# The second layer norm of an encoder block: root and bias moved to a diagonal matrix product on TensorE

## The chip, the core and the metric

One NeuronCore of a Trainium2 chip runs the whole program: TensorE (PE) with its weight loads (PEld), VectorE (DVE), ScalarE (ACT), GpSimd (POOL) and SyncE (SP), which issues most DMAs. The metric is the device time of one execution in microseconds (us), as the median of several runs.

## What is computed

One encoder block on 1024 tokens of width 1024: token mixer, first layer norm, a mixture of 32 experts with two per token, and a second layer norm. The change touches only the last step:

```python
def _layer_norm(x, gain, bias):
    xf = x.astype(jnp.float32)
    mu = jnp.mean(xf, axis=-1, keepdims=True)
    var = jnp.mean(jnp.square(xf - mu), axis=-1, keepdims=True)
    y = (xf - mu) * lax.rsqrt(var + LN_EPS)
    return (y * gain.astype(jnp.float32) + bias.astype(jnp.float32)).astype(x.dtype)

x = _layer_norm(ALPHA * x + ffn, ln2_gain[layer], ln2_bias[layer])
```

## The kernel before

The experts add their rows to the tensor Y in DRAM with indirect DMAs from GpSimd (`scatter`, L1101). When the last of these has landed, a loop over experts' overflow blocks (L1152) runs zero times here, and SyncE loads Y back as eight tiles `zs[0]` to `zs[7]` of 128 tokens by 1024 columns (L1257). From there to the end of the program only the second norm runs.

Each tile passes through these steps. The queues of ScalarE and VectorE keep the order in which the code writes them (`manual_schedule`).

- Statistics. For tiles 0 and 4 (`DVE_STATS`) VectorE takes them: two `bn_stats` (L1278), `bn_aggr` (L1279), and the epsilon added (L1280). For the six others ScalarE passes over the tile twice: `sums(j, 0)` (L1268, mean) and `sums(j, 1)` (L1270, sum of squares about the mean); both write their unused result into the output tile `o`. VectorE then makes the variance of it with one small instruction (L1282).
- Reciprocal root. `first_root` has ScalarE make a first guess from the bits of the variance with Exp (L154) and square it (L155); VectorE refines it with four instructions of one column, each reading the one before (two at L156, then L157 and L158). The result is -16/5 of the root, which the gain's factor of -5/16 (L1258) makes good.
- `centred` (L1294): VectorE subtracts the mean and multiplies by the gain, in place, over 1024 columns.
- `finish` (L1301): VectorE multiplies by the root and adds the bias over 1024 columns, and SyncE writes the tile out (L1302); the last tile goes in two halves.

The loop of L1310 to L1325 interleaves them: the centring of tile a, the first statistics pass of tile a+2 on ScalarE, the variance and first root step of tile a+1, the second pass of tile a+2, and the finish of tile a. TensorE has no work after the last expert. The PSUM tag `gu` has three buffers of 128 by 512.

A matrix product of plain float32 operands is used by the router (`logits`, L820: 128 by 128 against 36 columns, eight per token tile) and, as a transpose against the identity, at L813 and L1029. The large products (`mm3`, L162 to L164) use operands of type fp32r, three products per pair.

Of the kernel before, what the change touches and what calls it, by code (L numbers as in the profile page):

```python
# [11 lines left out]
F32 = mybir.dt.float32  # L12
F32R = mybir.dt.float32r
BF = mybir.dt.bfloat16
I32 = mybir.dt.int32
AF = mybir.ActivationFunctionType
OP = mybir.AluOpType
# [6 lines left out]
D = 1024  # L24
# [43 lines left out]
Y_OUT = (6, 7)  # L68
COMB = ()
M4 = 4  # L70
LN2_ORDER = tuple(range(8))
DVE_STATS = (0, 4)
LN2_LAST = 7


C_ID = 0
# [30 lines left out]
def body(tc, ctx, A, out):  # L107
    nc = tc.nc
    PE, ACT, DVE, POOL, SP = nc.tensor, nc.scalar, nc.vector, nc.gpsimd, nc.sync
# [11 lines left out]
    def nm(s):  # L121
        uid[0] += 1
        return f"{s}{uid[0]}"

    def slot(shape, dt, name):
        return S.tile([128] + shape, dt, name=nm(name), tag="S", bufs=NS)
# [7 lines left out]
    def st(shape, name="st", dt=F32):  # L134
        return sm.tile([128] + shape, dt, name=nm(name), tag="st", bufs=8)
# [7 lines left out]
    def r(ap):  # L143
        return ap.bitcast(F32)

    def split(hi, lo, src):
        ACT.copy(hi, src)  # L147
        DVE.tensor_sub(lo, src, r(hi))  # L148

    def rsqrt_steps(y, x, q):  # L150


        return [
            lambda: (ACT.activation(y, x.bitcast(I32), AF.Exp, scale=-0.5 * LN2 / 2 ** 23, bias=rs_b),  # L154
                     ACT.activation(q, y, AF.Square)),  # L155
            lambda: (DVE.tensor_mul(x, x, q), DVE.scalar_tensor_tensor(q, x, -4.2, x, op0=OP.add, op1=OP.mult)),  # L156
            lambda: (DVE.scalar_tensor_tensor(q, q, 7.0, x, op0=OP.add, op1=OP.mult),  # L157
                     DVE.scalar_tensor_tensor(y, q, -7.0, y, op0=OP.add, op1=OP.mult)),  # L158
        ]
# [9 lines left out]
    ident = cst[:, C_ID:C_ID + 128]  # L169
# [22 lines left out]
    raws, halves = {}, {}  # L192
# [39 lines left out]
    for k in range(8):  # L232
# [9 lines left out]
        for m in range(4):  # L242
            for h in range(2):
                c, t = slice(m * 128, m * 128 + 128), slice(h * 512, h * 512 + 512)
# [16 lines left out]
    ang, n = pf[:, 0], pf[:, 1]  # L261
# [32 lines left out]
    def F(shape, name="f"):  # L294
        n = cur["f"] = cur["f"] + 1
        settle(("f", n - cur["nF"]))
        return cur["F"].tile([128] + shape, F32, name=nm(name), tag="F", bufs=cur["nF"])
# [211 lines left out]
    q = SP.dma_start(TAB, A["tab"])  # L509
# [145 lines left out]
    steps = [(h, i) for h in range(NH) for i in range(8)]  # L655
# [3 lines left out]
    for s in range(-2, len(steps)):  # L659
        h, i = steps[max(s, 0)]  # L660
        b = B[i]
        if s >= 0 and h < NH - 1:
            q = (h + 1) // 2
# [66 lines left out]
    for m in range(8):  # L730
# [6 lines left out]
        for h in range(2):  # L737
            t = slice(h * 512, h * 512 + 512)
            if m % 3 == 0 or m >= M4:
                ps = F([512], "pa")  # L740
            else:
                if h == 0:
                    pa = p3.tile([128, T], F32, name=nm("pa"), tag="S", bufs=2)
                ps = pa[:, t]
            for _ in rows(ps, ("wa", m), h, oT, h):
                pass
            x = st([512], "mt")
# [17 lines left out]
    for i in range(8):  # L765
        b = where["wo", i]
        for h in range(2):
            k, n = i // 4 * 4 + i % 2 * 2 + h, i // 2 % 2
            c = slice(h * 512, h * 512 + 512)
# [195 lines left out]
    with tc.manual_schedule(engines={mybir.EngineType.PE, mybir.EngineType.Activation}):  # L965
        for group in ((0, 1), (2,), (3,), (4,), (5,), (6, 7)):
# [3 lines left out]
            i = 0  # L970
# [24 lines left out]
    def mt(shape, name, dt, bufs):  # L995
        return mo.tile([128] + shape, dt, name=nm(name), tag=name, bufs=bufs)

    def rt(shape, name, dt, bufs):
        return mt(shape, name, dt, bufs)[:CAP]

    def pt(shape, name, bufs, rows=128):
        return p6.tile([128] + shape, F32, name=nm(name), tag=name, bufs=bufs)[:rows]
# [17 lines left out]
    def turn_to(n, name):  # L1020
        return mt([2, n, CAP], name, F32R, {8: XT_BUFS, 4: HT_BUFS}[n])
# [180 lines left out]
    with tc.manual_schedule(engines={mybir.EngineType.PE, mybir.EngineType.Activation, mybir.EngineType.DVE}):  # L1202
        x, h = turn_to(8, "xT"), rt([512], "h", F32, 1)
# [5 lines left out]
        for e in range(NE):  # L1209
# [20 lines left out]
            if e == 0:  # L1230
                x = x1
            elif e + 1 < NE:
                x = turn_to(8, "xT")
# [12 lines left out]
    ln2 = slot([2, D], F32, "ln2")  # L1246
# [5 lines left out]
    zs = []  # L1252
    for j in range(8):
        if j % 2 == 0:
            zp = slot([2, D], F32, "z")
        zs.append(zp[:, j % 2])
        SP.dma_start(zs[j], Y[j * 128:j * 128 + 128])  # L1257
    ACT.activation(ln2[:, 0], ln2[:, 0], AF.Copy, scale=-5.0 / 16)  # L1258
    warm = mt([1], "warm", F32, 1)
    ACT.activation(warm, eps, AF.Exp)  # L1260
    os, vs = {}, {}

    def sums(j, i):

        if j not in DVE_STATS:
            v, o = vs[j], os[j // 2][:, j % 2]
            if i == 0:
                ACT.activation(o, zs[j], AF.Copy, scale=1.0 / D, accum_out=v[:, 0:1])  # L1268
            else:
                ACT.activation(o, zs[j], AF.Square, bias=v[:, 0:1], scale=-1.0, accum_out=v[:, 4:5])  # L1270

    def variance(j):
        z, v = zs[j], vs[j]
        var = v[:, 1:2]
        if j in DVE_STATS:
            b = mt([12], "bn", F32, 2)
            for h in range(2):
                DVE.bn_stats(b[:, 6 * h:6 * h + 6], z[:, 512 * h:512 * h + 512])  # L1278
            DVE.bn_aggr(v[:, 0:2], b)  # L1279
            DVE.tensor_scalar(var, var, EPS, None, op0=OP.add)  # L1280
        else:
            DVE.tensor_scalar(var, v[:, 4:5], 1.0 / D, EPS, op0=OP.mult, op1=OP.add)  # L1282

    def halves(j):
        n = 2 if j == LN2_LAST else 1
        return [slice(i * (D // n), (i + 1) * (D // n)) for i in range(n)]

    def first_root(j):
        v = vs[j]
        vs[j, "r"] = steps = rsqrt_steps(v[:, 2:3], v[:, 1:2], v[:, 3:4])  # L1290
        steps[0]()

    def centred(j):
        DVE.scalar_tensor_tensor(zs[j], zs[j], vs[j][:, 0:1], ln2[:, 0], op0=OP.subtract, op1=OP.mult)  # L1294

    def finish(j):
        o, y = os[j // 2][:, j % 2], vs[j][:, 2:3]
        for s in vs[j, "r"][1:]:
            s()
        for c in halves(j):  # L1300
            DVE.scalar_tensor_tensor(o[:, c], zs[j][:, c], y, ln2[:, 1, c], op0=OP.mult, op1=OP.add)  # L1301
            SP.dma_start(out[j * 128:j * 128 + 128, c], o[:, c])  # L1302

    for j in range(8):
        if j % 2 == 0:
            os[j // 2] = slot([2, D], F32, "o")
        vs[j] = mt([5], "v", F32, 8)

    with tc.manual_schedule(engines={mybir.EngineType.Activation, mybir.EngineType.DVE}):
        j = LN2_ORDER + (None, None)  # L1310
        variance(j[0])
        sums(j[1], 0)
        first_root(j[0])
        sums(j[1], 1)
        for a in range(8):
            centred(j[a])
            if a < 6:
                sums(j[a + 2], 0)
            if a < 7:
                variance(j[a + 1])  # L1320
                first_root(j[a + 1])
            if a < 6:
                sums(j[a + 2], 1)
            finish(j[a])
    p6p.__exit__(None, None, None)  # L1325


# [88 lines left out]
```

## Time and profile before

| | us |
|---|---|
| median of 3 runs (lowest, highest) | 1566.15 (1562.53, 1566.98) |
| the profiled execution's own time | 1564.77 |
| its span, first to last instruction | 1563.0 |
| PE busy in the span | 1488.5 (95%) |
| DVE busy | 1195.1 (76%) |
| ACT busy | 945.3 (60%) |
| POOL busy | 277.3 (18%) |
| chip's granted TensorE clock, mean | 0.976 of full speed |

All times of rows count from the span's start. Shares are of the whole span, and stages differ: for the change only the last 45 us matter, in which TensorE does nothing. A spacing is the time from the start of one instruction to the start of the next on the same engine; a row's duration can be a little longer than the spacing, since the end of one instruction overlaps the start of the next. The granted clock is 1.00 for 2.4 GHz and 0.50 for 1.2 GHz.

### The profile page before, as it was taken

How to read it: one execution, taken by the hardware profiler on the slowest of the kernel's cores; microseconds unless marked ns; L12 is line 12 of the kernel's file. 1: busy time of each engine (PE TensorE's matmuls, PEld its weight loads, DVE VectorE, ACT ScalarE, POOL GpSimd, SP SyncE). 2: the span in 40 equal slices, each digit the busy share in tenths (PEclk: the TensorE clock that was granted, in tenths of full speed). 3: DMA queues.
4: the chain of work that ended last, by engine and by line, in shares of the span. 5: the costliest groups of instructions: out<-in, count | busy, mean ns of one | idle time of the engine just before them, and what ended most of it. 6: DMA issues, size and time to landing. Idle time of an engine off the chain costs nothing.

```text
span 1563.0 us, 22004 instructions
## 1 busy us (share of the span) xinstructions
PE 1488.5 (95%) x7627; PEld 1189.5 (76%) x7627; DVE 1195.1 (76%) x2284; ACT 945.3 (60%) x1571; POOL 277.3 (18%) x231
## 2 busy tenths in 40 slices
PE   8999999999999999999999988999999999999980
PEld 6988887798798898888888775777777777776750
DVE  5774214987988987775566788999989999898967
ACT  4323124665666766674341116888888888888864
POOL 0001000220210211100002544223222222211410
PEclk9999999999999999999999988999999999999995
DMA  6156224746856765618465477999999999999945
GB/s 237 56 175 201 81 75 101 222 152 170 231 184 176 215 188 144 150 67 312 150 256 208 171 261 256 383 370 375 375 374 356 362 364 357 366 352 377 396 147 215
DMA packets 116977, 375.46 MB, mean 240 GB/s; under 512 B 13767, under 2 KB 44871, under 8 KB 91504
## 3 DMA queue, kind: packets, MB, share of 16 engines
q1 hardware_dynamic: 76128, 303.25, 52.7%
q0 software_dynamic: 40160, 69.96, 17.3%
q8 instruction: 61, 1.00, 0.3%
q10 hardware_dynamic: 576, 0.83, 0.2%
q14 instruction: 52, 0.43, 0.1%
HBM read 312.44 MB, written 69.78 MB: 245 GB/s over the span
## 4 chain that ended last, share of the span: by engine, by line
PE 55%; issue 28%; POOL 9%; DVE 5%; ACT 1%; DMA 1%; POOLq 0%; DVEq 0%; SPq 0%; ACTq 0%
POOL Y L1101 7%; PE ps L570 4%; PE pg L162 4%; PE pg L163 4%; PE pg L164 4%; PE po L621 3%; PE pv L162 2%; PE pv L164 2%; PE pv L163 2%; PE tp L606 2%; POOL xg L1089 2%; PE pa L164 2%; PE pa L163 2%; PE pa L162 2%; PE pw L162 2%
## 5 line engine op out<-in xcount | busy, mean ns | idle before, releaser
L148 DVE TENSOR_TENSOR wh<-we,wh 128x1024 fp32r<-128x1024 f32 x384 | 459.7, 1219 | 54.1 <-ACT wh L147 50.5
L147 ACT CAST wh<-we 128x1024 fp32r<-128x1024 f32 x384 | 400.4, 1047 | 90.0 <-PE gu L164 51.5
L162 PE MATMUL gu<-wh,xT 128*96 128x512 f32 x512 | 204.3, 399 | 0.0
L164 PE MATMUL gu<-wh,xT 128*96 128x512 f32 x512 | 202.6, 396 | 0.6 <-DVE xT L148 0.6
L163 PE MATMUL gu<-wh,xT 128*96 128x512 f32 x512 | 201.8, 394 | 0.0
L1101 POOL DMA_INDIRECT Y<-y,idx x32 | 108.5, 3390 | 265.4 <-ACT y L1109 260.6
L148 DVE TENSOR_TENSOR w<-wraw,w 128x512 fp32r<-128x512 f32 x111 | 75.7, 685 | 92.1 <-ACT w L147 91.7
L147 ACT CAST w<-wraw 128x512 fp32r<-128x512 f32 x111 | 68.5, 621 | 115.1 <-PE pg L164 36.4
L573 ACT ACTIVATE P<-ps,stat 128x256 f32<-128x256 f32 (+7 forms) x128 | 94.8, 741 | 58.9 <-DVE stat L572 58.4
L164 PEld LDWEIGHTS gu<-wh,xT 128*96 128x96 f32 x512 | 83.0, 162 | 37.2 <-DVE xT L148 1.3
L163 PEld LDWEIGHTS gu<-wh,xT 128*96 128x96 f32 x512 | 83.3, 163 | 34.1 <-issue 0.5
L162 PEld LDWEIGHTS gu<-wh,xT 128*96 128x96 f32 x512 | 83.0, 162 | 33.2 <-ACT xT L147 0.2
L162 PE MATMUL dn<-wh,hT 128*96 128x512 f32 x256 | 102.4, 400 | 0.6 <-ACT hT L147 0.6
L570 PE MATMUL ps<-K,Q 128*128 128x512 f32 (+2 forms) x384 | 99.5, 364 | 1.2 <-DVE z L461 0.8
L164 PE MATMUL dn<-wh,hT 128*96 128x512 f32 x256 | 100.6, 393 | 0.0
L163 PE MATMUL dn<-wh,hT 128*96 128x512 f32 x256 | 100.6, 393 | 0.0
L162 PE MATMUL pg<-xT,w 128*128 128x512 f32 x256 | 100.4, 392 | 0.0
L163 PE MATMUL pg<-xT,w 128*128 128x512 f32 x256 | 100.0, 391 | 0.0
L164 PE MATMUL pg<-xT,w 128*128 128x512 f32 x256 | 99.9, 390 | 0.0
L572 DVE TENSOR_REDUCE stat<-ps 128x1 f32<-128x256 f32 (+7 forms) x128 | 95.3, 746 | 1.1
L570 PEld LDWEIGHTS ps<-K,Q 128*128 128x128 f32 x384 | 64.6, 189 | 10.8 <-DVE z L461 1.3
L162 PE MATMUL pv<-w,xT 128*128 128x256 f32 x256 | 72.8, 284 | 0.0
(277 smaller groups left out, 3395.3 us busy)
## 6 DMA issues: line engine op xcount, KB each, us to landing
we<-in_we_dram SPq DMA_DIRECT2D x192, 1024.0 KB, 23.5
wraw<-in_w_dram SPq DMA_DIRECT2D x61, 512.0 KB, 3.8
Q<-RQ POOLq DMA_DIRECT2D x64, 256.0 KB, 5.2
RQ<-rh SPq DMA_DIRECT2D x32, 256.0 KB, 3.3
K<-RK POOLq DMA_DIRECT2D x16, 512.0 KB, 5.5
V<-RV POOLq DMA_DIRECT2D x16, 512.0 KB, 5.7
OT<-ohl SPq DMA_DIRECT2D x48, 128.0 KB, 2.5
oT<-OT POOLq DMA_DIRECT2D x6, 1024.0 KB, 12.1
```

Of the source, the lines that this page charges most:

```text
L147: ACT.copy(hi, src)
L148: DVE.tensor_sub(lo, src, r(hi))
L162: PE.matmul(ps, a[0], b[0], start=start, stop=False)
L163: PE.matmul(ps, a[0], b[1], start=False, stop=False)
L164: PE.matmul(ps, a[1], b[0], start=False, stop=stop)
L570: PE.matmul(ps[:, c:c + n], q[:, o, m, qc], Kt[h, m][:, c:c + n], start=o == 0, stop=o == 1)
L572: DVE.tensor_reduce(st_[:, m:m + 1], ps[:, :W], AX.X, OP.max, negate=True)
L573: ACT.activation(Pt[h, i][m][:, :W], ps[:, :W], AF.Exp, bias=st_[:, m:m + 1], accum_out=st_[:, 2 + m:3 + m])
L606: PE.transpose(ps[:, k], p[:, (4 * g + k) * 128:(4 * g + k) * 128 + 128], ident)
L621: PE.matmul(o[:, 0, c], Vt[h][:, a, kt], aT[kt // 4][:, kt % 4, b, c], start=j == 0, stop=j == len(parts) - 1)
L1089: q = POOL.indirect_dma_start(out=x, out_offset=None, in_=X1, in_offset=IO(ap=idx[:, int(e < NXG), expert[e]:expert[e] + 1], axis=0), boun ...
L1101: q = POOL.indirect_dma_start(out=Y, out_offset=IO(ap=idx[:, 0, expert[e]:expert[e] + 1], axis=0), in_=y, in_offset=None, bounds_check=T - ...
```

## The change

Three things are changed in the second norm, and nothing before it.

- The statistics are shared four to four: VectorE takes those of tiles 0, 2, 4 and 6, ScalarE those of 1, 3, 5 and 7.
- For tiles 1 to 6 the multiplication by the root and the bias leave VectorE. ScalarE writes a 128 by 128 matrix with the root on its diagonal (the identity times the column y). TensorE makes each half tile of 512 columns in a PSUM buffer of the tag `gu` as two products of a row of ones with the bias row (split into two fp32r parts) and one float32 product of the diagonal matrix with the centred tile. ScalarE copies the two halves to `o`, and SyncE writes the tile out in one DMA. Tiles 0 and 7 stay with VectorE, in two halves each.
- The four refining instructions of the root are spread: the first is issued at the start of an iteration, the second ahead of another tile's centring, the last two behind it.

Ahead of the loop the bias row is split (a ScalarE copy and a VectorE subtraction on one partition) and a row of ones is made (VectorE). The queue of TensorE is now in written order in this stage too.

```diff
-LN2_ORDER = tuple(range(8))
-DVE_STATS = (0, 4)
-LN2_LAST = 7
+DVE_STATS = (0, 2, 4, 6)
+DVE_SCALED = (0, 7)
...
     ACT.activation(ln2[:, 0], ln2[:, 0], AF.Copy, scale=-5.0 / 16)
+    bias = slot([2, D], F32R, "bias")[:1]
+    split(bias[:, 0], bias[:, 1], ln2[:1, 1])
+    lone = slot([128], F32R, "lone")[:1]
+    DVE.tensor_scalar(lone, ident[:1], 0.0, 1.0, op0=OP.mult, op1=OP.add)
+    diags = slot([2, 128], F32, "diag")
...
-    def finish(j):
-        o, y = os[j // 2][:, j % 2], vs[j][:, 2:3]
-        for s in vs[j, "r"][1:]:
-            s()
-        for c in halves(j):
-            DVE.scalar_tensor_tensor(o[:, c], zs[j][:, c], y, ln2[:, 1, c], op0=OP.mult, op1=OP.add)
-            SP.dma_start(out[j * 128:j * 128 + 128, c], o[:, c])
+    def scaled(j):
+        y = vs[j][:, 2:3]
+        if j in DVE_SCALED:
+            for c in halves:
+                DVE.scalar_tensor_tensor(os[j][:, c], zs[j][:, c], y, ln2[:, 1, c], op0=OP.mult, op1=OP.add)
+                SP.dma_start(out[j * 128:j * 128 + 128, c], os[j][:, c])
+            return
+        diag = diags[:, j % 2]
+        ACT.activation(diag, ident, AF.Copy, scale=y)
+        norm_ps[j] = [pt([512], "gu", 3) for c in halves]
+        for ps, c in zip(norm_ps[j], halves):
+            for k in range(2):
+                PE.matmul(ps, lone, bias[:, k, c], start=k == 0, stop=False)
+            PE.matmul(ps, diag, zs[j][:, c], start=False, stop=True)
+
+    def taken_out(j):
+        if j not in DVE_SCALED:
+            for ps, c in zip(norm_ps[j], halves):
+                ACT.copy(os[j][:, c], ps)
+            SP.dma_start(out[j * 128:j * 128 + 128], os[j])
...
-        j = LN2_ORDER + (None, None)
-        variance(j[0])
-        sums(j[1], 0)
-        first_root(j[0])
-        sums(j[1], 1)
-        for a in range(8):
-            centred(j[a])
-            if a < 6:
-                sums(j[a + 2], 0)
-            if a < 7:
-                variance(j[a + 1])
-                first_root(j[a + 1])
-            if a < 6:
-                sums(j[a + 2], 1)
-            finish(j[a])
+        for a in range(-3, 9):
+            def of(i, f, *n):
+                if 0 <= a + i < 8:
+                    f(a + i, *n)
+
+            of(1, root, 1)
+            of(0, scaled)
+            of(3, sums, 0)
+            of(2, variance)
+            of(2, root, 0)
+            of(-1, taken_out)
+            of(3, sums, 1)
+            of(1, root, 2)
+            of(2, centred)
+            of(1, root, 3)
+            of(1, root, 4)
```

Here `root(j, 0)` is the Exp and the square on ScalarE, and `root(j, 1)` to `root(j, 4)` are the four VectorE instructions.

## Rows read from the trace of the kernel before

**Rows 1.** Windows: length; busy us of PE, PEld, DVE, ACT, POOL; clock, DMA share, GB/s
```profile
1540.00:1545.00 5.00, 0.00 (x0) 0.00 (x0) 4.79 (x13) 1.55 (x5) 0.00 (x0) 0.50 0.47 190
```
**Rows 2.** Chain of waits in order of time: start, us, what; the norm's beginning
```profile
1524.93 4.46 DMA z<-Y
...
1533.56 0.15 DVE v L1282
...
1534.40 1.28 DVE o L1301
```
**Rows 3.** Timeline of the norm, VectorE: start, duration, line, operation, tiles, count
```profile
1537.62 1.28 DVE L1301 SCALAR_TENSOR_TENSOR o<-z,v,ln 128x1024 f32<-128x1024 f32 x1
...
1538.82 1.28 DVE L1294 SCALAR_TENSOR_TENSOR z<-z,v,ln 128x1024 f32<-128x1024 f32 x1
...
1540.85 1.29 DVE L1301 SCALAR_TENSOR_TENSOR o<-z,v,ln 128x1024 f32<-128x1024 f32 x1
...
1543.24 1.28 DVE L1278 BATCH_NORM_STATS2 bn<-z 128x6 f32<-128x512 f32 x2
...
1545.64 1.28 DVE L1301 SCALAR_TENSOR_TENSOR o<-z,v,ln 128x1024 f32<-128x1024 f32 x1
```
**Rows 4.** Timeline of the norm, ScalarE: one tile's passes and another's first root step
```profile
1533.44 1.04 ACT L1268 ACTIVATE o<-z 128x1024 f32<-128x1024 f32 x1
...
1534.47 0.28 ACT L154 ACTIVATE v<-v,rs_b 128x1 f32<-128x1 int32 x1
...
1534.79 0.20 ACT L155 ACTIVATE v<-v 128x1 f32<-128x1 f32 x1
1534.90 1.13 ACT L1270 ACTIVATE o<-z,v 128x1024 f32<-128x1024 f32 x1
...
1536.03 1.04 ACT L1268 ACTIVATE o<-z 128x1024 f32<-128x1024 f32 x1
```
**Rows 5.** By line and shape, whole span, ScalarE: busy us, mean ns, idle before
```profile
L580 ACT ACTIVATE P<-P,stat 128x128 f32<-128x128 f32 x8 | 3.2, 400 | 3.8 <-DVE stat L579 3.8
```
**Rows 6.** Timeline of ScalarE at the router: two PSUM halves copied out
```profile
840.29 1.08 ACT L814 COPY xT<-px 128x512 f32<-128x512 f32 x2 [6.87 <-PE px L813]
```
**Rows 7.** By line and shape, whole span, TensorE: the router's float32 products
```profile
L820 PE MATMUL pr<-wr,xT 128*128 128x36 f32 x128 | 17.4, 296 | 2.2 <-ACT xT L814 1.8 <-DVE first L899 0.4
```
**Rows 8.** Timeline of TensorE as the experts begin: float32 transposes, then fp32r products
```profile
946.87 1.54 PE L1029 MATMUL X<-cst,xg 96*128 96x96 f32 x8 [5.96 <-DMA xg<-X,idx]
948.34 0.74 PE L162 MATMUL gu<-wh,xT 128*96 128x512 f32 x1
...
951.87 0.63 PE L164 MATMUL gu<-wh,xT 128*96 128x512 f32 x1
952.29 0.63 PE L162 MATMUL gu<-wh,xT 128*96 128x512 f32 x1
...
953.05 0.39 PE L164 MATMUL gu<-wh,xT 128*96 128x512 f32 x1
953.28 0.39 PE L162 MATMUL gu<-wh,xT 128*96 128x512 f32 x1
...
954.67 0.82 PE L1029 MATMUL X<-cst,xg 96*128 96x96 f32 x8
```
**Rows 9.** Windows by clock (columns as in rows 1): router's end, and after the last expert
```profile
929.00:934.00 5.00, 5.00 (x24) 4.65 (x24) 4.45 (x20) 1.47 (x3) 3.91 (x3) 0.50 1.01 407
...
1519.00:1520.00 1.00, 0.00 (x0) 0.00 (x0) 0.00 (x0) 0.00 (x0) 0.75 (x1) 0.77 0.03 8
```
**Rows 10.** Timeline of VectorE: the last tile's two output halves
```profile
1558.49 1.41 DVE L1301 SCALAR_TENSOR_TENSOR o<-z,v,ln 128x512 f32<-128x512 f32 x2
```
**Rows 11.** Output DMAs: count, KB each, median us from issue to landing
```profile
out_dram<-o SPq DMA_DIRECT2D x7, 512.0 KB, 2.6
out_dram<-o SPq DMA_DIRECT2D x2, 256.0 KB, 2.0
```
**Rows 12.** Timeline of ScalarE, last expert: the idle time ahead of an eviction
```profile
1514.60 0.68 ACT L1109 ACTIVATE y<-dn,first 96x512 f32<-96x512 f32 x1 [1.76 <-PE dn L164]
```

More of the change, by code (lines that the diff above doesn't have):

```diff
@@ L1258, in body @@
     ACT.activation(ln2[:, 0], ln2[:, 0], AF.Copy, scale=-5.0 / 16)
+    bias = slot([2, D], F32R, "bias")[:1]
+    split(bias[:, 0], bias[:, 1], ln2[:1, 1])
+    lone = slot([128], F32R, "lone")[:1]
+    DVE.tensor_scalar(lone, ident[:1], 0.0, 1.0, op0=OP.mult, op1=OP.add)
     warm = mt([1], "warm", F32, 1)
     ACT.activation(warm, eps, AF.Exp)
-    os, vs = {}, {}
+    diags = slot([2, 128], F32, "diag")
+    os, vs, norm_ps = [], [], {}
     def sums(j, i):
         if j not in DVE_STATS:
-            v, o = vs[j], os[j // 2][:, j % 2]
+            v, o = vs[j], os[j]
             if i == 0:
@@ L1282, in variance, with root @@
             DVE.tensor_scalar(var, v[:, 4:5], 1.0 / D, EPS, op0=OP.mult, op1=OP.add)
[L1284 to L1288, printed above, removed]
+    def root(j, i):
         v = vs[j]
-        vs[j, "r"] = steps = rsqrt_steps(v[:, 2:3], v[:, 1:2], v[:, 3:4])
-        steps[0]()
+        y, x, q = v[:, 2:3], v[:, 1:2], v[:, 3:4]
+        if i == 0:
+            rsqrt_steps(y, x, q)[0]()
+        elif i == 1:
+            DVE.tensor_mul(x, x, q)
+        elif i == 2:
+            DVE.scalar_tensor_tensor(q, x, -4.2, x, op0=OP.add, op1=OP.mult)
+        elif i == 3:
+            DVE.scalar_tensor_tensor(q, q, 7.0, x, op0=OP.add, op1=OP.mult)
+        else:
+            DVE.scalar_tensor_tensor(y, q, -7.0, y, op0=OP.add, op1=OP.mult)
@@ L1304, in body @@
+    def taken_out(j):
[3 more added lines that the diff above has]
+            SP.dma_start(out[j * 128:j * 128 + 128], os[j])
+    halves = [slice(0, 512), slice(512, 1024)]
     for j in range(8):
         if j % 2 == 0:
-            os[j // 2] = slot([2, D], F32, "o")
-        vs[j] = mt([5], "v", F32, 8)
-    with tc.manual_schedule(engines={mybir.EngineType.Activation, mybir.EngineType.DVE}):
-        j = LN2_ORDER + (None, None)
-        variance(j[0])
-        sums(j[1], 0)
-        first_root(j[0])
-        sums(j[1], 1)
-        for a in range(8):
-            centred(j[a])
-            if a < 6:
-                sums(j[a + 2], 0)
-            if a < 7:
-                variance(j[a + 1])
-                first_root(j[a + 1])
-            if a < 6:
-                sums(j[a + 2], 1)
-            finish(j[a])
+            op_ = slot([2, D], F32, "o")
+        os.append(op_[:, j % 2])
+        vs.append(mt([5], "v", F32, 8))
@@ new lines, in body @@
+    with tc.manual_schedule(engines={mybir.EngineType.PE, mybir.EngineType.Activation, mybir.EngineType.DVE}):
+        for a in range(-3, 9):
[13 more added lines that the diff above has]
+            of(1, root, 4)
```

## The prediction

> **What bounds the kernel now.** I read the windows of the last stretch first, then the chain of waits back from the end, then the timeline of each engine there. The windows show the norm as a VectorE stage: of 5 us VectorE is busy 4.79, ScalarE 1.55, TensorE not at all [rows 1]. The chain shows how it begins: the tiles' load, ScalarE's two passes over tile 1, its variance at 1533.56, and from the output of tile 0 at 1534.40 on nothing but VectorE until the end [rows 2]. So what a tile costs is what VectorE spends on it. From one tile's output to the next is 3.23 us (1537.62 to 1540.85): output 1.20, centring 1.20, and 0.83 for the variance and the four dependent root steps. Where VectorE takes the statistics too it is 4.79 us (1540.85 to 1545.64), so that these cost 1.56 us [rows 3]. A pair of tiles is 6.46 us, or 8.02 with statistics for one.
>
> The end itself: the last two output halves take 1.41 us from 1558.49, to 1559.90 [rows 10], and half a tile lands 2.0 us after its issue [rows 11]. With 0.05 us from engine to queue the last bytes land at 1561.95. I compare this landing with the one of the changed kernel; the 1.05 us from there to the end of the span of 1563.0 and the 1.8 us from the span to the profiled run's own 1564.77 stay. That run lies 1.4 us below the median of 1566.15, within the spread of the three.
>
> **Removed from VectorE.** Six outputs of 1.20 us: 7.2 us. Spreading the root steps puts a long instruction between steps that now wait for each other; I credit it with 0.33 us a tile (0.83 less about 0.50 for variance, four steps and one wait that is left), an estimate bounded by zero and 0.4. **Added to VectorE:** statistics of two more tiles, 2 x 1.56 = 3.1 us. As queue work alone VectorE would thus save some 4.1 us, and up to 6.7 with the spread steps.
>
> **ScalarE's queue** loses two tiles' statistics (each 1.03 for the mean pass and 1.13 for the squares, as spacings [rows 4]): 4.3 us. For each of six tiles it gains the diagonal matrix, 0.40 us by the nearest shape [rows 5] and about 0.30 as spacing, since ends overlap starts by some 0.1 (the square at 1534.79 lasts 0.20, the next starts at 1534.90 [rows 4]); and two copies out of PSUM, 1.08 for two [rows 6], 0.98 as spacing. Exp and square of the root stay, 0.43 [rows 4]. A pair costs it 1.03 + 1.13 + 2 x (0.43 + 0.30 + 0.98) = 5.58 us. That is less than VectorE's 6.46 before, so by queue sums alone either engine would gain.
>
> **TensorE** gets per half tile two fp32r products with the bias and one float32 product, all of 512 columns. The fp32r spacing is 0.23 us at 2.4 GHz and 0.42 at 1.2 GHz [rows 8]. A float32 product of 512 columns isn't in the trace. Below, it is two records (the router's 64 products left 128 [rows 7]) at the fp32r spacing, 0.46 us. Above, two records at the column rate of a float32 transpose: eight of 96 columns take 0.82 us warm and 1.54 cold, the last record's own length (0.25 and 0.42) taken off and divided by 7 that is 0.08 and 0.16 for 96 columns [rows 8], so 0.44 and 0.86 for 512, and 0.88 and 1.75 for two records. I take the upper value, as the transposes have the operand type and the identity matrix of the new product. A tile then costs 4 x 0.23 + 2 x 0.88 = 2.68 us warm and 4 x 0.43 + 2 x 1.75 = 5.2 us cold (1.84 and 3.5 by the lower value). It starts cold: 2 us after the last expert the clock has fallen [rows 9].
>
> **Where the gain goes: a ring.** In the written order the three queues wait for one another. On ScalarE the second statistics pass of an odd tile stands behind two things: the Exp of an even tile, which waits for VectorE's statistics of it, and the copies of an earlier tile. On VectorE the variance of the odd tile, with the centring queued behind it and then the next even tile's statistics, waits for that pass. One turn serves two tiles: Exp and square 0.43, copies 0.98, squares pass 1.13 and 0.12 until VectorE has its sum, then on VectorE variance 0.07, a root step 0.08, centring 1.20, the last two steps 0.27 and the next tile's first 0.08, statistics and variance 1.56 + 0.07 and 0.12 of latency: 6.1 us. Against the 6.46 of a pair before, the six outputs taken off VectorE buy 0.3 us a turn, and more (1.9) only where the old order had statistics on VectorE as well.
>
> **The schedule, laid by these spacings.** Until 1533.56 nothing changes. VectorE then centres tile 1 before it finishes tile 0 and takes tile 2's statistics: variance 0.07, a root step 0.08, centring 1.20, two root steps 0.27, tile 1's first 0.08, two output halves 1.32, statistics and variance 1.63, latency 0.12: tile 2's variance is out at about 1538.3. ScalarE, done with the mean pass of tile 3 at about 1535.1, waits 3.2 us for it. Square and squares pass of tile 3 end at 1539.8; tile 1's root is ready at 1539.8 and its diagonal matrix at 1540.25. TensorE begins there, cold: product 1.75, bias 0.86, product 1.75, with 0.3 until ScalarE sees it 1545.0, half a microsecond after ScalarE wanted it. ScalarE then copies, and passes over tile 5 until 1546.8. One VectorE part of the ring (3.5 with its latency) gives tile 6's variance at 1550.25; exp, copies of tile 3 and the squares of tile 7 end at 1552.8. Tile 5's matrix is next, 1553.2; TensorE is warm by then: its two halves (0.88 + 0.46 + 0.88) end at 1555.4. Tile 6 follows without a gap, since its matrix is ready at 1555.1: 0.46 + 0.88 + 0.46 + 0.88, 1558.1, with 0.17 of latency 1558.3. The last copy (0.61 with its latency) ends at 1558.9, and a whole tile lands 2.6 us after its issue [rows 11]: 1561.6. VectorE has tile 7 done at 1556.7, which isn't late. Against 1561.95 that is 0.4 us earlier. The profiled 1564.77 becomes 1564.4; carried to the median, **1565.8 us**.
>
> The small edits have one answer. The bias row's copy, about 1.05 us on ScalarE, fits into the 1.76 us that ScalarE idles ahead of an eviction [rows 12], or into the wait for the tiles; VectorE's subtraction and row of ones fall there too. If the copy came ahead of the last expert's splits, it would cost 1 to 2 us.
>
> **Rivals.**
>
> *The clock never rises* (slower). TensorE is first used after 20 us of idleness, and float32 work alone has left it at 1.2 GHz: from 929 to 934 TensorE was busy all 5 us with float32 transposes and router products at a granted 0.50 [rows 9]. It decides from the point where a tile on TensorE costs more than half a turn of the ring, 3.05 us: warm it is 2.68, cold 5.2. Then TensorE is the bound from 1540.25 on: 12 products of 1.75 and 11 pairs of bias products of 0.85 end at 1570.6, with the latency, the copy and the landing 1574, and with the ring's own stalls at the end about 1575. That is 13 us more: **1579 us** (by the lower product price 3 us more, 1569). Against it: the fp32r products at 948.34 brought the clock up by 953.05 [rows 8], and TensorE will stream 512 columns a record without a gap while it is behind; the router's products have 36. The Trainium skill (TensorE: Matmul & The Clock Gate, Part 4: PE-mode transpose) says that transposes don't count as work that releases the clock; if the chip took the float32 diagonal products the same way, this rival would be the result. The row of 929 to 934 agrees with that sentence, but has no long float32 product in it. Chance 0.14.
>
> *The float32 product has the lower price* (0.46 us warm): the ring is never kept waiting, and the last two tiles take 0.84 us each less on TensorE; the same schedule lands at 1559.6, 2.3 us less: **1563.8 us**. For it: the two records; against it: the transposes' column rate. Chance 0.10.
>
> *The queues hardly wait for one another*, and VectorE's work saved comes through in full, 4.1 to 6.7 us: **about 1561 us**. The written order speaks against it. Chance 0.05.
>
> *The bias split delays the last expert*: **1567.5 us**. Chance 0.03.
>
> **How the numbers follow.** The forecast, no change, has 0.68: 1564 to 1569, as a clock that rises 4 us later costs 1.7 us, one at 2.4 GHz from the start gains 0.7, and runs of the kernel before differ by 4 us. About 0.3% (4.7 us) is what a measurement of this kernel can tell from no change. Faster by more than that needs the third rival or a part of the second: 0.06. Slower needs the cold clock at the upper price: 0.15. The rest, 0.79, is the same. The range takes in the second rival less the spread below, and the cold clock at the lower price with the spread above: 1562 to 1571; it leaves out the cold clock at full price and the full saving.
>
> **What would show it.** Right: a period of about 6.1 us per two tiles after 1541; ScalarE idle some 3 us ahead of the Exp of tile 2; VectorE idle ahead of the variance of tiles 5 and 7; TensorE's float32 records spaced 0.44 us by the end and 0.87 at the start; tile 6, out of PSUM, landing last. Wrong: a granted clock of 0.50 to the end with ScalarE waiting for TensorE at every copy; records of 0.23 us; VectorE without waits and busy over 90%; any change before 1528.

## The result: 18 us slower

The changed kernel takes 1582.43 us in the median (1580.72 to 1585.31, four runs) against 1566.38 for the kernel before in the same runs; the ratio is 1.0115, with a 95% interval of 1.0091 to 1.0139, so 14 to 22 us more (16 by the medians, 18 by the ratio). The forecast was 1565.8 (1562 to 1571), no change. It was wrong; what happened is the rival "the clock never rises", to which the prediction gave 0.14 and 1579 us.

The profiled execution has a span of 1579.0 us. The first load of the norm's tiles is issued at 1522.29 in it and at 1524.52 in the kernel before; how early the experts end varies by some 4 us from run to run whatever the norm does (1522.29 to 1526.69 in all traces of this case). I therefore compare the stretch from that issue to the end of the span and call it the tail: 38.48 us before, 56.71 after, 18.2 us more. Each tail is read from one execution.

The windows answer to rows 1 and 9 (columns as there):

```profile
1530.00:1535.00 5.00, 0.00 (x0) 0.00 (x0) 3.98 (x11) 2.65 (x6) 0.00 (x0) 0.50 0.95 382
1540.00:1545.00 5.00, 5.00 (x8) 1.95 (x8) 2.54 (x9) 3.55 (x9) 0.00 (x0) 0.50 0.08 31
1550.00:1555.00 5.00, 5.00 (x8) 1.50 (x6) 0.16 (x1) 2.41 (x7) 0.00 (x0) 0.50 0.26 105
1565.00:1570.00 5.00, 5.00 (x8) 2.00 (x8) 0.00 (x0) 1.17 (x2) 0.00 (x0) 0.50 0.15 56
```

From 1540 on TensorE is busy without a break, and the granted clock stays at 0.50 to the end. VectorE, 4.79 of 5 us busy in rows 1, is nearly idle in two of these windows. The chain of waits (start, us, what) is TensorE from the first diagonal product to the last:

```profile
1537.60 0.30 ACT diag L1316
1537.90 0.04 issue
1537.94 2.08 PE gu L1321 x2
1540.02 1.15 PE gu L1320 x2
1541.17 2.01 PE gu L1321 x2
...
1572.70 2.02 PE gu L1321 x2
1574.72 0.02 issue
1574.74 0.59 ACT o L1326
```

A half tile is two records of the diagonal product (L1321) and two one-row bias products (L1320): 2.01 + 1.15 = 3.15 us, 6.3 a tile, twelve halves. In the view of waits (who waited for whom: us in total, times, longest) the other engines stand behind that:

```profile
ACT o L1326 <- PE gu L1321: 21.0, 11, 2.6
...
DVE v L1287 <- ACT o L1275: 8.9, 3, 5.5
```

### The profile page after: what moved, and what is told of

Its sections match the earlier page's. It is cut to its first block, busy times and chain, and to the rows that moved or that the text cites. A ratio compares the mean times of both kernels' runs of the same rounds, so it can differ in the third digit from the quotient of the medians.

```text
span 1579.0 us, 22118 instructions
## 1 busy us (share of the span) xinstructions
PE 1525.9 (97%) x7675; PEld 1200.8 (76%) x7675; DVE 1190.5 (75%) x2287; ACT 951.2 (60%) x1582; POOL 278.5 (18%) x231
## 4 chain that ended last, share of the span: by engine, by line
PE 57%; issue 27%; POOL 9%; DVE 4%; ACT 1%; DMA 1%; POOLq 0%; SPq 0%; ACTq 0%; DVEq 0%
POOL Y L1100 7%; PE ps L569 4%; PE pg L161 4%; PE pg L162 4%; PE pg L163 4%; PE po L620 3%; PE pv L161 2%; PE pv L163 2%; PE pv L162 2%; PE tp L605 2%; POOL xg L1088 2%; PE pa L161 2%; PE pa L163 2%; PE pa L162 2%; PE pB L161 2%
```

## The experiments

### Without the TensorE part

```diff
-DVE_SCALED = (0, 7)
+DVE_SCALED = tuple(range(8))
```

> The changed kernel with all eight tiles multiplied by the root and given the bias on VectorE, so that TensorE, the diagonal matrices and the copies out of PSUM are gone; statistics shared four to four and spread root steps stay. If the TensorE products alone make the kernel slow, the time falls from 1582.4 to near that of before: VectorE's queue holds two more statistics (+3.1 us) and the spread steps (-1.3 to -2.6 us), so 1566 to 1568 us. If the new order of the queues is at fault, it stays above 1575 us.

Measured: 1565.8 us, ratio 1.0007 (0.9993 to 1.0022). The tail is 40.17 us, 1.7 longer than before. The statistics shared four to four and the spread root steps cost next to nothing; the loss lies in the TensorE part. (This result and two below, without the bias and the last of all, lie 0.2 to 0.7 us under their expected ranges. The kernel before was lower too in those experiments, 1563.89 and 1564.82 us in the median against 1566.38, so the ratios decide.) The 1.7 us fit the sums: two more statistics on VectorE (3.1 us) against what the spread steps give back.

### The clock brought up beforehand

```diff
+    full = slot([2, D], F32R, "bias")
+    split(full[:, 0], full[:, 1], ln2[:, 1])
+    bias = full[:1]
...
+            if j == 1 and c is halves[0]:
+                idle = pt([512], "dn", 2)
+                for _ in range(32):
+                    PE.matmul(idle, full[:, 0, :128], full[:, 0, :512], start=True, stop=True)
```

> The changed kernel with 32 extra fp32r products of 128 rows by 512 columns, read by nobody, on TensorE ahead of the first diagonal product (for their operand the bias is split on all 128 partitions, which takes the engines as long as on one). They fill TensorE's idle time from 1528 to 1538 and should bring the clock to 2.4 GHz by about 1533. Theory 1, the cold start is all that is wrong and the norm's own products keep the clock up: granted 1.00 to the end, float32 records spaced 0.45 to 0.5 us, the ring of the three queues binds, 1565 us (1564 to 1567). Theory 2, these products do not count as enough work: the clock falls back to 0.50 some us after 1538 and the time is 1577 to 1582 us.

Measured: 1566.22 us, ratio 1.0011 (1.0001 to 1.0021). The timeline of TensorE, then two windows:

```profile
1530.92 10.05 PE L1325 MATMUL dn<-bias 128*128 128x512 f32 x32
1540.80 1.02 PE L1326 MATMUL gu<-z,diag 128*128 128x512 f32 x2
1541.75 0.73 PE L1321 MATMUL gu<-bias,lone 1*128 1x512 f32 x2
1542.41 1.13 PE L1326 MATMUL gu<-z,diag 128*128 128x512 f32 x2
1543.46 0.73 PE L1321 MATMUL gu<-bias,lone 1*128 1x512 f32 x2
1544.12 1.13 PE L1326 MATMUL gu<-z,diag 128*128 128x512 f32 x2
```
```profile
1535.00:1540.00 5.00, 5.00 (x21) 4.03 (x20) 4.76 (x14) 2.19 (x7) 0.00 (x0) 0.88 0.40 149
1555.00:1560.00 5.00, 5.00 (x13) 1.77 (x12) 0.96 (x2) 1.75 (x3) 0.00 (x0) 1.00 0.53 210
```

Once at 2.4 GHz the clock stays there through the norm's own products, the same ones that never raised it. The clock is worth some 16 us: the tail is 41.17 us, against 56.71. But a half tile costs 1.71 us even so (1542.41 to 1544.12), 3.4 a tile, more than the 1.34 and 2.68 of the forecast, and TensorE is without a pause to the end: it sets the pace, where the expectation had the ring of the three queues do so. About 1 us of the tail belongs to the experiment itself, as the 32 products end that much after the first diagonal matrix is ready.

### Without the bias, and with a bias of 128 rows

The first leaves the bias products out. The second gives them 128 rows, each a 128th of the bias:

```diff
-            for k in range(2):
-                PE.matmul(ps, lone, bias[:, k, c], start=k == 0, stop=False)
-            PE.matmul(ps, diag, zs[j][:, c], start=False, stop=True)
+            PE.matmul(ps, diag, zs[j][:, c], start=True, stop=True)
```
```diff
-    lone = slot([128], F32R, "lone")[:1]
-    DVE.tensor_scalar(lone, ident[:1], 0.0, 1.0, op0=OP.mult, op1=OP.add)
+    bias = full
+    lone = slot([128], F32R, "lone")
+    DVE.tensor_scalar(lone, ident, 0.0, 1.0 / 128, op0=OP.mult, op1=OP.add)
```

> The products of the row of ones with the bias are left out (the bias is missing from tiles 1 to 6); TensorE runs float32 diagonal products alone, without a pause between them while it is behind. Theory A, the one-row products are what keeps the clock low (they fill 1.15 of every 3.15 us): the clock rises to 1.00 within some us of 1542, records are spaced about 0.5 us, and the time is 1563 to 1567 us. Theory B, the float32 diagonal products themselves do not raise the clock: granted 0.50 to the end, records spaced 1.0 us, 4.0 us of TensorE a tile, last product at about 1562, time 1566 to 1571 us.

> The bias products have 128 rows instead of one (128 by 128 matrix of 1/128 against the bias row on all partitions; same output). Theory A, the one-row products are what keeps the clock low: it rises to 1.00 some us after 1540 and the time is 1563 to 1568 us. Theory B, the float32 products are at fault: the bias products are too few to matter, granted 0.50 to the end, 1580 to 1584 us as the changed kernel.

Measured: 1562.35 us (ratio 0.9982, 0.9969 to 0.9995) without the bias, and 1564.12 us (0.9997, 0.9984 to 1.001) with 128 rows. The clock comes up in both; without the bias:

```profile
1545.00:1550.00 5.00, 4.08 (x9) 1.53 (x9) 4.62 (x14) 4.65 (x14) 0.00 (x0) 0.94 0.51 203
```

and with 128 rows:

```profile
1540.00:1545.00 5.00, 4.80 (x9) 2.59 (x10) 4.72 (x15) 3.67 (x11) 0.00 (x0) 0.64 0.00 0
1545.00:1550.00 5.00, 5.00 (x17) 2.96 (x16) 3.83 (x12) 4.64 (x13) 0.00 (x0) 1.00 0.52 206
```

The weight loads (PEld) of the run without the bias, each starting with its record, show the spacing of float32 records before and after the clock rises:

```profile
1541.36 0.34 PEld L1319 LDWEIGHTS gu<-z,diag 128*128 128x128 f32 x1 [0.52 <-issue]
1542.21 0.34 PEld L1319 LDWEIGHTS gu<-z,diag 128*128 128x128 f32 x1 [0.52 <-issue]
...
1545.62 0.19 PEld L1319 LDWEIGHTS gu<-z,diag 128*128 128x128 f32 x1 [0.51 <-ACT diag L1316]
1546.05 0.19 PEld L1319 LDWEIGHTS gu<-z,diag 128*128 128x128 f32 x1 [0.24 <-issue]
```

So neither the float32 form nor the zeros of a diagonal matrix keep the clock down: float32 diagonal products by themselves raise it. The one-row products, placed between them as in the changed kernel, prevent it. With them widened, this is the kernel that the forecast described, its tail 37.58 us, 0.9 shorter than before (forecast: 0.4).

Why TensorE needs 3.15 us a half shows in the weight loads at the changes between bias and diagonal products. With one row such a load starts only as its own product starts; with 128 rows it runs under the product before. (A row with x2 holds two loads or two products and starts with the first; the second load of a pair runs under the pair's first product in both kernels.) The changed kernel's timeline:

```profile
1546.25 0.50 PEld L1320 LDWEIGHTS gu<-bias,lone 1*128 1x128 f32 x2 [1.50 <-ACT v L154]
1546.26 1.22 PE L1320 MATMUL gu<-bias,lone 1*128 1x512 f32 x2
...
1547.40 0.50 PEld L1321 LDWEIGHTS gu<-z,diag 128*128 128x128 f32 x2 [0.65 <-issue]
1547.40 1.22 PE L1321 MATMUL gu<-z,diag 128*128 128x512 f32 x1
```

and that of the kernel with 128 rows:

```profile
1545.03 1.03 PE L1322 MATMUL gu<-bias,lone 128*128 128x512 f32 x2
...
1545.66 0.42 PEld L1323 LDWEIGHTS gu<-z,diag 128*128 128x128 f32 x2
...
1545.89 1.02 PE L1323 MATMUL gu<-z,diag 128*128 128x512 f32 x2
```

The load of the diagonal matrix starts at the same 1547.40 as its product in the first, and 0.23 us ahead in the second. There a half tile takes 1.32 us (1545.03 to 1546.35), the forecast's 1.34. Four records at their spacing of 0.85 and 0.43 us would make 2.56 us a half at 1.2 GHz; the 0.59 more in the changed kernel are two late loads of some 0.3 us. The windows count this time as busy, since a product's record starts with its load.

### 32 rows and 96 rows

```diff
-    bias = full
-    lone = slot([128], F32R, "lone")
-    DVE.tensor_scalar(lone, ident, 0.0, 1.0 / 128, op0=OP.mult, op1=OP.add)
+    bias = full[:32]
+    lone = slot([128], F32R, "lone")[:32]
+    DVE.tensor_scalar(lone, ident[:32], 0.0, 1.0 / 32, op0=OP.mult, op1=OP.add)
```

and the same with 96.

> The bias products have 32 rows (1/32 against the bias row on 32 partitions; same output): between the changed kernel's one row and the 128 of the run before. Theory A1, the clock looks at how many rows work: a quarter of the array for 0.86 of 2.6 us is nearly as little as one row, granted 0.50 to the end, 1576 to 1583 us. Theory A2, it is the exposed weight loads (PEld and PE start together at every product beside a one-row one) that leave TensorE empty, and they come from the operands' unlike row counts: exposed here too, 0.50 to the end. Theory A3, only the one-row form is special: weight loads hidden, clock up by about 1545, 1563 to 1566 us as with 128 rows.

> Bias products of 96 rows (1/96 against the bias row on 96 partitions), between the run with 32, where the clock stayed low, and that with 128. If a difference in the row count alone makes each next weight load late, the loads are late here too and, if that is what keeps the clock low, it stays at 0.50: 1578 to 1583 us. If loads are late and the clock rises all the same, the number of working rows decides: a half tile then costs 1.7 us as in the run with the clock brought up beforehand, 1565 to 1569 us. If no load is late, 1563 to 1566 us.

Measured: 1580.91 us with 32 rows (ratio 1.0105, 1.0081 to 1.0129), 1564.8 us with 96 (1.0005, 0.9994 to 1.0017). With 32 rows loads and products start together and the clock stays at 0.50, in every way as with one row:

```profile
1541.18 0.50 PEld L1323 LDWEIGHTS gu<-z,diag 128*128 128x128 f32 x2 [0.65 <-issue]
```
```profile
1560.00:1570.00 10.00, 10.00 (x14) 3.44 (x14) 1.41 (x2) 2.06 (x4) 0.00 (x0) 0.50 0.21 82
```

With 96 rows the loads run ahead and the clock comes up, as with 128:

```profile
1545.37 0.42 PEld L1323 LDWEIGHTS gu<-z,diag 128*128 128x128 f32 x2
1545.60 1.02 PE L1323 MATMUL gu<-z,diag 128*128 128x512 f32 x2
```

So an unlike row count doesn't by itself make a load late; 32 against 128 does, 96 against 128 doesn't. Late loads and a low clock went together here, which leaves open whether the few rows or the broken stream of products keep the clock down.

### Short one-row products, and one-row products in groups

The first shortens the bias products to 64 columns, so that the bias is missing from the other 448 of each half:

```diff
-            for k in range(2):
-                PE.matmul(ps, lone, bias[:, k, c], start=k == 0, stop=False)
-            PE.matmul(ps, diag, zs[j][:, c], start=False, stop=True)
+            PE.matmul(ps, diag, zs[j][:, c], start=True, stop=False)
+            for k in range(2):
+                PE.matmul(ps[:, :64], lone, bias[:, k, c][:, :64], start=False, stop=k == 1)
```

The second puts a tile's four bias products together:

```diff
                 PE.matmul(ps, lone, bias[:, k, c], start=k == 0, stop=False)
+        for ps, c in zip(norm_ps[j], halves):
             PE.matmul(ps, diag, zs[j][:, c], start=False, stop=True)
```

> Bias products of one row as in the changed kernel, but on 64 of the 512 columns and behind the diagonal product (the bias is missing from the other 448 columns of each half of tiles 1 to 6). The changes between one-row and 128-row products are as many as in the changed kernel, with their late weight loads; the time in one-row products is an eighth. If the time in which few rows of TensorE work keeps the clock low, it now rises within some us of 1543, float32 records are spaced 0.43 us and the time is 1563 to 1567 us. If the late weight loads at each change do it, the clock stays at 0.50, a half tile costs about 2.3 us and the time is 1568 to 1573 us.

> One-row bias products as in the changed kernel, but the four of a tile stand together ahead of its two diagonal products, so that TensorE changes between one-row and 128-row products twice a tile instead of four times; nothing else differs. Late loads at the changes: two fewer a tile, about 0.3 us each way, 5.7 instead of 6.3 us a tile at 0.50, 1577 to 1580 us. If the clock rises with fewer changes: 1563 to 1567 us.

Measured: 1577.04 us with short products (ratio 1.008, 1.0053 to 1.0106), above the range of either theory, as a half costs 2.57 us (1542.31 to 1544.88) and not 2.3; 1566.27 us grouped (1.0021, 1.0005 to 1.0036). With short ones the clock stays at 0.50 to the end:

```profile
1560.00:1570.00 10.00, 10.00 (x17) 3.73 (x16) 0.78 (x2) 2.64 (x5) 0.00 (x0) 0.50 0.40 157
```

Grouped, it stays at 0.50 for three tiles and then rises (timeline, then windows):

```profile
1550.41 3.78 PE L1322 MATMUL gu<-z,diag 128*128 128x512 f32 x4
1554.13 1.22 PE L1320 MATMUL gu<-bias,lone 1*128 1x512 f32 x4
1555.27 1.98 PE L1322 MATMUL gu<-z,diag 128*128 128x512 f32 x4
```
```profile
1550.00:1555.00 5.00, 5.00 (x10) 1.86 (x8) 0.16 (x1) 2.18 (x7) 0.00 (x0) 0.58 0.25 99
1555.00:1560.00 5.00, 5.00 (x14) 2.01 (x12) 3.60 (x11) 3.56 (x9) 0.00 (x0) 1.00 0.52 208
```

Before the rise a tile takes 5.71 us (1544.70 to 1550.41) instead of 6.3, so that two changes fewer save 0.3 us each. This profiled execution, at 1569.4 us, is a late one among its eight runs (1564.67 to 1570.53); the clock rose in all eight, as their mean granted clock is 0.979 to 0.984 against 0.970 to 0.973 in the four of the changed kernel. The pair of runs speaks against the time in one-row products as the cause: with an eighth of it the clock stays low, with all of it, but half as many changes between few and many rows, the clock rises. What the low runs share is a stream broken four times a tile by late weight loads. That fits every kernel here whose norm starts TensorE cold, but it isn't shown to be the cause: a kernel with late loads and full rows alone, which would settle it, wasn't tried.

### ScalarE's order, and two other divisions

```diff
-            of(-1, taken_out)
             of(3, sums, 1)
+            of(-1, taken_out)
```

The second kernel adds `DVE_STATS = (0, 1, 6)` and `DVE_SCALED = (0, 3, 6, 7)` to it, both with the bias of 128 rows. The third is the kernel without the TensorE part with `DVE_STATS = (0, 1)`.

> Bias products of 128 rows, and on ScalarE the second statistics pass of an odd tile ahead of the copies out of PSUM instead of behind them. If the ring of the forecast binds (copies 0.98 us of a 6.1 us turn), two tiles take 5.1 us and the time falls 1 to 2 us below the run with 128 rows, to about 1562 us. If ScalarE's work as a whole and TensorE's last two tiles bind, nothing changes: 1564 us.

> Bias products of 128 rows, order as in the run before, VectorE's statistics for tiles 0, 1 and 6 and its outputs for tiles 0, 3, 6 and 7, so that TensorE and the diagonal matrices serve four tiles instead of six and none at the end. Laid out by the spacings of the traces the last bytes land at 1556 to 1557.5 where the kernel before has 1561.95: 1560 to 1562 us, 0.3% faster than before. If the waits between the queues eat it again, 1563 to 1565 us.

> No TensorE in the norm: all outputs on VectorE, its statistics for tiles 0 and 1 alone (so that no engine waits for ScalarE's first two passes), root steps spread. Laid out by the spacings of the traces the landing is 3.5 us ahead of the kernel before: two statistics as before, the wait of 2.5 us for tile 1 filled, the spread steps worth 0.1 to 0.3 us a tile. 1561 to 1563 us. If the spread steps give nothing, about 1564 us.

Measured: 1563.98 us for the order (ratio 1.0001, 0.9989 to 1.0012), 1560.59 us for the division with TensorE (0.9978, 0.9966 to 0.999), 1560.49 us for the one without (0.998, 0.9969 to 0.9991). The tails are 38.01, 34.77 and 35.45 us, against 38.48 before.

The order is worth nothing in time, although the ring does turn faster. On ScalarE's timeline two tiles, from the Exp of tile 4 to that of tile 6, take 6.18 us with the old order (1543.30 to 1549.48) and 5.63 with the new one (1545.74 to 1551.37):

```profile
1543.30 0.30 ACT L153 ACTIVATE v<-v,rs_b 128x1 f32<-128x1 int32 x1 [0.26 <-DVE v L1287]
...
1549.48 0.30 ACT L153 ACTIVATE v<-v,rs_b 128x1 f32<-128x1 int32 x1 [0.26 <-DVE v L1287]
```
```profile
1545.74 0.29 ACT L153 ACTIVATE v<-v,rs_b 128x1 f32<-128x1 int32 x1 [0.26 <-DVE v L1287]
...
1551.37 0.28 ACT L153 ACTIVATE v<-v,rs_b 128x1 f32<-128x1 int32 x1
```

What is gained comes back as waits for TensorE at the end: the last halves leave PSUM 1.33 us apart, TensorE's pace.

```profile
1557.83 0.59 ACT L1328 COPY o<-gu 128x512 f32<-128x512 f32 x1 [0.74 <-PE gu L1323]
1559.16 0.58 ACT L1328 COPY o<-gu 128x512 f32<-128x512 f32 x1 [0.74 <-PE gu L1323]
1560.48 0.58 ACT L1328 COPY o<-gu 128x512 f32<-128x512 f32 x1 [0.74 <-PE gu L1323]
```

The other two are faster than the kernel before by 0.2%. The one without TensorE reaches it by keeping VectorE busy nearly all the time (9.90 of 10 us):

```profile
1540.00:1550.00 10.00, 0.00 (x0) 0.00 (x0) 9.90 (x27) 7.63 (x18) 0.00 (x0) 0.50 0.43 158
```

VectorE takes the statistics of tile 1, for whose variance it waited 2.5 us in the kernel before (timeline there):

```profile
1533.56 0.15 DVE L1282 TENSOR_SCALAR v<-v 128x1 f32<-128x1 f32 x1 [2.50 <-ACT o L1270]
```

And as ScalarE's first instruction is now an Exp, its table load falls into the wait for the tiles, the first of which has statistics taken from 1526.29 on (timeline of this run):

```profile
1522.79 1.28 ACT L153 ACT_TABLE_LOAD   x1 [6.71 <-issue]
```

## Why the prediction was wrong

The step that failed is "TensorE is warm by then", in the schedule, and the reason against the rival: that TensorE would stream records of 512 columns without a gap while it is behind. It was behind and busy in every window, but its stream was broken at each change between one-row and 128-row products, and the clock stayed at 0.50 for the 37 us that it was needed. The evidence I weighed, the float32 work of 929 to 934 at 0.50 [rows 9] against the fp32r start of the experts [rows 8], differed in the wrong respect: I asked whether float32 counts, where the one-row products mattered, which had no row at all. That they are what kept the clock down is shown by the runs without them and with 128 rows; whether by the late loads or otherwise stays open. The bias products should have been a term with bounds of its own; I gave them the price and the effect of a 128-row product.

The Trainium skill's sentence (TensorE: Matmul & The Clock Gate, Part 4: PE-mode transpose) that transposes do not release the clock doesn't carry over to float32 diagonal products: without the bias they brought it up (granted 0.94 from 1545 to 1550).

The rival's price was 13 us; the tail grew by 18.2. A half tile at 1.2 GHz was put at 2.61 us and took 3.15, since the loads at its two changes came late by some 0.3 us each (the spacings measured make 2.56 us without them); over eleven and a half halves the 0.54 us are 6.2 us. Against it stands 1 us that the rival had added for stalls of the ring: TensorE's chain has none. TensorE's start (priced at 15.7 us after the loads' first issue, measured 15.65) and its float32 product were right: records are spaced 0.85 us cold and 0.43 warm in the run without the bias, against 0.87 and 0.44 from the transposes.

What held, seen in the kernel with 128 rows:

- The gain of six outputs off VectorE is eaten by the ring: a turn of 6.18 us for two tiles (forecast 6.1), and 0.9 us less in the tail (forecast 0.4). ScalarE waits for tile 2's variance as put down, in the changed kernel 3.03 us.

```profile
1535.94 0.29 ACT L153 ACTIVATE v<-v,rs_b 128x1 f32<-128x1 int32 x1 [3.03 <-DVE v L1285]
```

- That the ring binds alone was too strong: ScalarE's sum for a pair (5.58) and TensorE's last tiles stand close behind it, as the changed order showed.
- The small edits cost nothing, though not where I put them. The copy of the bias ran after the last expert, at 1522.44, in the wait for the tiles. Its subtraction, 1.1 us, stood between tile 0's statistics and their last step while ScalarE made its first pass over tile 1; the variance was out at 1528.41 even so, and the Exp that reads it started at 1529.45, behind ScalarE's table load.

## What to carry to other kernels

Before work is moved to an idle TensorE, price it at 1.2 GHz as well, and ask which of its products could keep the clock from rising; 24 one-row products between 12 full ones cost some 18 us here, and the same bias written with 128 rows nothing. Count the queues that a tile crosses: what is taken off the busiest engine comes back as waits when the same tile has to pass VectorE, ScalarE, TensorE and ScalarE again. A change of which tile goes where, with no new engine, gave more (0.2%) than the new engine did.

## What the runs showed of the hardware

- The granted clock depends on its past: the same products of TensorE ran at 0.50 to the end from a cold start (37 us) and at 1.00 to the end when 32 fp32r products went ahead.
- At a change of row count, weight loads ran under the product before where the counts were 96 and 128 (0.23 us ahead of their own product, as with 128 and 128), and started only with their own product where they were 1 or 32 and 128. The Trainium skill (TensorE: Matmul & The Clock Gate, Part 3, "What overlaps and what doesn't") says that a load overlaps a running product only when the row groups differ, though the text above that list also names a background weight buffer; here loads for the same 128 rows did overlap, and the measurement decides against the list.
- A float32 product of 128 rows by 512 columns is two records, 0.85 us apart at 1.2 GHz and 0.43 at 2.4 GHz, about twice the spacing of fp32r records of the same size (0.42 and 0.23 [rows 8]).
